# Hybrid attention, FFN and PLE layer: differential steps, the PLE gate and the order of three engines rearranged

## The chip, the core and the metric

The kernel runs on one core of one Trainium2 chip. The metric is device microseconds (us) of one execution. TensorE (PE in the profile) multiplies matrices, VectorE (DVE), ScalarE (ACT) and GpSimd (POOL) work on elements, SyncE (SP) and POOL issue DMA transfers. Each engine works through its own list of instructions in order, and semaphores make one wait for another.

## The reference

One layer on 512 tokens of 1024 features, all fp32. Cut to what matters:

```python
h = rms_norm(x, attn_norm_g); z = h @ w_in       # q, kv latents, rope key | diff q, k, v
x = x + concat[MLA heads (8 x 64), differential heads (4 x 128)] @ w_out
x = x + conv_ffn(rms_norm(x, ffn_norm_g), w_gate, w_up, conv_w, conv_b, w_down)   # D_FF = 2816
gate = jax.nn.sigmoid(rms_norm(x, ple_norm_g) @ w_ple_gate)                       # 1024 x 1024
x = x + gate * (p @ w_ple_proj)
...
probs = jax.nn.softmax(logits, axis=-1)          # differential head: two maps of one head
attn = (probs[:, :, 0] - lam * probs[:, :, 1])
return jnp.einsum('bhqk,bhkd->bhqd', attn, v_t)
```

Attention is causal by chunks of 64 tokens, so query block t (128 tokens) sees key blocks 0 to t.

## The kernel before

**Layout.** Everything is kept transposed: features on the 128 partitions, the 512 tokens on the free axis. The residual x is eight blocks of 128 features by 512 tokens. W_out, the FFN and the gate each give output blocks of that shape.

**Three matmuls for one.** For accuracy each operand is kept as a high half rounded to fp32r and a low half with the rest. mm3 (L188) issues three matmuls: high by high (L191), weight's high by activation's low (L192), weight's low by activation's high (L193). Weights are split when they have been loaded: ACT casts the high half (hi_, L1021), DVE subtracts for the low one (lo_, L1026; hl does both). split (L216) does the same for activations.

**Order.** PE runs the matmuls as the program's text lists them, written out by hand so that PE always has something ready. The other engines' order from MLA step 4 to the first FFN blocks is permuted afterwards by the table ISSUE (L69), one list of numbers for each of DVE, ACT, POOL and SP, which in_order (L228) applies to what has been traced since a mark. Behind that point the order is that of the text.

**The differential steps** (L960) go over 16 slots, head h and query block t. A slot issues logits two slots ahead (diff_qk, diff_soft, diff_comb), a filling product of W_out (pump, of FILL_DIFF's number of units), the transposes of its own P (probs_T, L591, tile pTd), P times V of the slot before (diff_pv, tile do), transposes of a later head's q and k (diff_T, tiles d0T and so on), and at some slots the split of a finished head's output (y_split, tile yT).

**The FFN** works through 22 blocks of 128 hidden features. From block 3 on, gate and up are computed together by a seven-product scheme on half blocks (gu_units, L1256; product, L1252): instead of eight products of half of the features by half of the tokens it takes seven, of sums of weights and sums of tokens, and adds the results. The sums of weights are made by an accumulating DMA on POOL's queue (w_sums, L1133; tile rS), the sums of tokens on DVE (tokens, L1169). Down products (down_units, L1336, tile dn) fill in between, and add_x (L738) adds each to x.

**The tail.** The last two groups of hidden blocks are multiplied by dn4 and dn5 (L1486, L1490), eight output blocks. As each block of x is ready, norm_in (L1481) splits it, times the gain, into h3h and h3l, and squares it for the norm (square, L1048: ACT squares, DVE sums into ss). Then the gate: pg (L1512) multiplies one output block, 8 feature blocks by 3 matmuls, 512 tokens wide, the last output block in two halves of 256. The first two output blocks take their first four feature blocks before the norm's matmul (L1538, with a square of ones, 512 wide; rms_v, L201, turns it into 1/rms in 11 DVE operations), since the factor 1/rms is only needed in ple_out (L1522): sg = pg times 1/rms, sigmoid on ACT, times the PLE projection ppi (loaded from DRAM, where an earlier stage wrote it), plus x, and out by DMA. Four 512 KB weight tiles of the gate are split early into FFN buffers (b1, b2), four late (pg_weights, L1509).

Of the kernel before, what the change touches and what calls it, by code (L numbers as in the profile page):

```python
# [128 lines left out]
def hybrid_block(ctx: ExitStack, tc: tile.TileContext, a: dict, out: bass.AP):  # L129
# [1308 lines left out]
    pump(2)  # L1438
    old, g = g, new
    for f in range(NPLAIN + 2, NF):  # L1440
# [13 lines left out]
        else:  # L1454
# [3 lines left out]
            pgw = []  # L1458
            for n, i in (("b1", 0), ("b2", 2)):
                h_, l_ = (ffn2.tile([P, 2, 1024], F32R, tag=n + j, name=f"pg{n}{j}") for j in "hl")  # L1460
                for j in range(2):
                    split(h_[:, j], l_[:, j], raw_w(a["w_pg"][i + j, 0], "rS", f"pg{i + j}", bufs=3))
                    pgw.append((h_[:, j], l_[:, j]))
# [170 lines left out]
```

## Time and profile before

| | us |
|---|---|
| median of 3 runs | 633.38 (633.19 to 633.41) |
| the profiled execution | 633.87 |
| its span (first to last instruction) | 632.1, mean granted clock 0.998 |
| busy: PE / PEld / DVE / ACT / POOL | 626.0 / 555.0 / 481.9 / 359.1 / 69.9 |
| moved by DMA | 82.63 MB |

PE is TensorE's matmuls, PEld its weight loads, which overlap them. A row of the trace gives an instruction's start, its length, its engine, its line, the operation, output and inputs by the program's tile names (their numbers left out), and in brackets how long the engine waited just before and for what. Lengths of neighbouring matmuls overlap, so the distance between starts says what one costs. A row of the windows gives the stretch, its length, then busy time and number of instructions of PE, PEld, DVE, ACT and POOL, then the mean granted clock, the DMA engines' busy share and GB/s.

### The profile page before, as it was taken

The numbers are of one execution on the slowest core, as the hardware profiler recorded it, in microseconds if no ns is written. First come the engines' busy times: TensorE is split into PE (matmuls) and PEld (weight loads), VectorE is DVE, ScalarE is ACT, GpSimd is POOL, SyncE is SP. The second block draws the span as 40 slices with busy tenths as digits, with TensorE's granted clock in tenths as the row PEclk, the third lists the DMA queues.
The fourth block names the chain that finished last, engine by engine and source line by source line (L and its number), as shares of the span: only waits on it lengthen the run. The fifth ranks groups of instructions, "written<-read, shape, count | busy, mean of one in ns | idle before, by whom it ended". The sixth has DMA issues, their size and how long they took to land.

```text
span 632.1 us, 10195 instructions
## 1 busy us (share of the span) xinstructions
PE 626.0 (99%) x3900; PEld 555.0 (88%) x3900; DVE 481.9 (76%) x870; ACT 359.1 (57%) x629; POOL 69.9 (11%) x94
## 2 busy tenths in 40 slices
...
GB/s 298 113 167 34 184 101 67 67 121 81 122 14 68 83 121 326 137 99 218 151 184 118 184 119 184 120 187 120 186 120 188 122 156 128 173 134 71 32 81 51
DMA packets 29912, 82.63 MB, mean 131 GB/s; under 512 B 3100, under 2 KB 4124, under 8 KB 29736
## 3 DMA queue, kind: packets, MB, share of 16 engines
...
q10 hardware_dynamic: 432, 0.49, 0.3%
...
## 4 chain that ended last, share of the span: by engine, by line
PE 98%; DMA 1%; ACT 0%; DVE 0%; ACTq 0%; issue 0%
PE dn L192 6%; PE dn L191 6%; PE dn L193 6%; PE gx L192 4%; PE gx L193 4%; PE gx L191 4%; PE g L191 4%; PE g L192 4%; PE g L193 4%; PE zd L191 4%; PE zd L193 4%; PE zd L192 3%; PE o L191 3%; PE u L191 2%; PE o L193 2%; PE o L192 2%
## 5 line engine op out<-in xcount | busy, mean ns | idle before, releaser
L1027 DVE TENSOR_TENSOR wSl<-rS,wSh 128x1024 fp32r<-128x1024 f32 x21 | 25.7, 1223 | 42.3 <-ACT wSh L1023 42.2
L191 PE MATMUL dn<-ah,hi_dn 128*128 128x512 f32 x144 | 56.3, 391 | 0.0
L192 PE MATMUL dn<-al,hi_dn 128*128 128x512 f32 x144 | 56.3, 391 | 0.0
L193 PE MATMUL dn<-ah,lo_dn 128*128 128x512 f32 x144 | 56.1, 389 | 0.0
L1136 POOL DMA_DIRECT2D rS<-in_w_gu x19 | 22.7, 1195 | 247.7 <-DVE cv L1304 129.1
L1023 ACT CAST wSh<-rS 128x1024 fp32r<-128x1024 f32 x21 | 22.0, 1048 | 37.3 <-PE gy L192 37.2
L191 PE MATMUL zd<-hi_d,xh 128*128 128x512 f32 x96 | 39.4, 411 | 0.0
L192 PE MATMUL zd<-lo_d,xh 128*128 128x512 f32 x96 | 37.6, 392 | 0.0
L739 DVE TENSOR_TENSOR x<-x,dn 128x512 f32<-128x512 f32 x44 | 29.8, 680 | 6.1 <-PE dn L193 6.1
L1023 ACT CAST wAh<-rA 128x1024 fp32r<-128x1024 f32 x21 | 22.1, 1052 | 20.0 <-DMA rA<-in_w_gu 12.3
L193 PEld LDWEIGHTS dn<-ah,lo_dn 128*128 128x128 f32 x144 | 27.1, 188 | 5.7
L1027 DVE TENSOR_TENSOR wTl<-rA,wTh 128x1024 fp32r<-128x1024 f32 x19 | 23.3, 1224 | 11.2 <-ACT wTh L1023 10.7
L191 PEld LDWEIGHTS dn<-ah,hi_dn 128*128 128x128 f32 x144 | 27.1, 188 | 5.1
L192 PEld LDWEIGHTS dn<-al,hi_dn 128*128 128x128 f32 x144 | 27.1, 188 | 5.0
L1027 DVE TENSOR_TENSOR wAl<-rA,wAh 128x1024 fp32r<-128x1024 f32 x21 | 25.6, 1217 | 4.5 <-ACT wAh L1023 4.5
L1307 ACT ACTIVATE cv<-cv 128x512 f32<-128x512 f32 x22 | 13.8, 630 | 25.6 <-DVE cv L1304 25.6
L191 PE MATMUL o<-yh,hi_o 128*128 128x512 f32 x64 | 26.8, 419 | 0.0
L192 PE MATMUL g<-b2l,wAh 128*128 128x256 f32 (+1 forms) x88 | 26.2, 298 | 0.0
L193 PE MATMUL g<-b2h,wAl 128*128 128x256 f32 (+1 forms) x88 | 26.2, 298 | 0.0
L191 PE MATMUL g<-b2h,wAh 128*128 128x256 f32 (+1 forms) x88 | 26.2, 298 | 0.0
L1527 ACT ACTIVATE sg<-sg 128x512 f32<-128x512 f32 (+1 forms) x9 | 5.3, 584 | 36.8 <-DVE sg L1526 36.8
L660 ACT ACTIVATE pm<-ml,sums,rq 128x128 f32<-128x128 f32 (+3 forms) x32 | 19.6, 617 | 9.8 <-DVE sums L636 6.1
...
## 6 DMA issues: line engine op xcount, KB each, us to landing
rA<-in_w_gu SPq DMA_DIRECT2D x22, 512.0 KB, 3.7
rS<-in_w_gu SPq DMA_DIRECT2D x22, 512.0 KB, 3.6
rS<-in_w_gu POOLq DMA_DIRECT2D x19, 512.0 KB, 6.0
raw_dn<-in_w_down SPq DMA_DIRECT2D x18, 512.0 KB, 5.8
raw_d<-in_w_d SPq DMA_DIRECT2D x12, 512.0 KB, 3.4
r<-in_w_gu SPq DMA_DIRECT2D x19, 256.0 KB, 5.8
raw_o<-in_w_out SPq DMA_DIRECT2D x8, 512.0 KB, 3.6
rS_pg<-in_w_pg SPq DMA_DIRECT2D x6, 512.0 KB, 4.1
```

What stands on the lines that cost most here:

```text
L191: TE.matmul(ps, xh, wh, start=first and i == 0, stop=False, skip_group_check=again)
L192: TE.matmul(ps, xh, wl, start=False, stop=False, skip_group_check=again)
L193: TE.matmul(ps, xl, wh, start=False, stop=last and i == n - 1, skip_group_check=again)
L660: S.activation(pm[c], ps[c], AF.Exp, bias=nm[:, c:c + 1], scale=r[:, c:c + 1], accum_out=sums[:, 1, c:c + 1])
L739: V.tensor_tensor(xb(b), xb(b), ps, op=ALU.add)
L1023: S.copy(h_, src)
L1027: V.tensor_tensor(l_, src, _f32(h_), op=ALU.subtract)
L1136: nc.gpsimd.dma_start(sums[f].rearrange("p (i c) -> p i c", i=2), a["w_gu"][f][:, :2048].rearrange("p (i c) -> p i c", i=2)[:, :, :512], a ...
L1307: S.activation(cv, cv, AF.Silu)
L1527: S.activation(sg, sg, AF.Sigmoid)
```

## The change

**The gate in seven products.** The gate's four pairs of output blocks (k and k + 4) are each computed by the scheme of the FFN. With the weight in four quarters, the tokens in two halves t1 and t2, and features in two halves (h1, blocks 0 to 3; h2, blocks 4 to 7), a pair takes the products named 11, 12, S2, S1, S3, S4 and 22, each four feature blocks by three matmuls, 256 tokens wide. 336 half matmuls take the place of 168 full and 48 half ones. The order on PE is: 11 of blocks 0 and 1, the norm's first part, 12 and 11 in turn for the rest, the norm's second part; then for each pair S2, S1, S3, S4, 22. Output block k is in pg, k + 4 in pu.

**What feeds it.** Host arrays hold w_pg in the layout of w_gu. For each k the sums of weights come by three accumulating transfers on POOL's queue behind loads on SP's: pg_sums (512 KB) makes the operand of S1 and S3, pg_mix (a load and two transfers of 256 KB, one after the other) that of S2 and S4, called t0 to t3. Weights are split twelve times at 1024 columns and four times at 512, in place of eight times at 1024. pg_tokens makes the sums of tokens: for each k four DVE operations on half blocks, two ACT casts and two DVE subtractions on full ones.

**The norm** uses norm_r and norm_b, which the first FFN norm has already: four matmuls of one column, a power on POOL, and one full matmul that spreads the result.

**The output.** Blocks 0, 1, 2, 4 and 5 are added into x by an accumulating DMA on POOL's queue; 3, 6 and 7 by DVE as before; 3 and 7, the last pair, go in two halves. ple_out's scalar -1 turns the sign of the upper blocks. ppi is loaded early (pp_in).

**The rest of the tail.** The last FFN block's product 22 now stands ahead of the last down unit (next(old), pump()); the last down weights are split into the tile btl.

**The differential steps.** P's transposes go ahead of the filling product, except at eight slots (early), and where no product is in the way; six slots change. P times V of the slot before moves to the slot's end. At slot (2,0), head 2 and query block 0, PE's rows before were (dl are logits, o the filling product, pTd P's transposes, do P times V):

```order
L193 MATMUL dl_2225<-st 128x384
L191 MATMUL o_2200<-yh_1857,hi_o_1948 128x512
L192 MATMUL o_2200<-yh2l,hi_o_1948 128x512
L193 MATMUL o_2200<-yh_1857,lo_o_1949 128x512
L191 MATMUL o_2200<-yh_1849,hi_o_1948 128x512
L192 MATMUL o_2200<-yh3l,hi_o_1948 128x512
L193 MATMUL o_2200<-yh_1849,lo_o_1949 128x512
L595 MATMUL pTd_2252<-ident,pmd 128x128
L817 MATMUL do_2119<-zd_1458,pt 128x128
```

And now (d0T are transposes of the next head's keys):

```order
L213 MATMUL dl_2225<-st 128x384
L615 MATMUL pTd_2245<-ident,pmd 128x128
L211 MATMUL o_2200<-yh_1857,hi_o_1948 128x512
L212 MATMUL o_2200<-yh2l,hi_o_1948 128x512
L213 MATMUL o_2200<-yh_1857,lo_o_1949 128x512
L211 MATMUL o_2200<-yh_1849,hi_o_1948 128x512
L212 MATMUL o_2200<-yh3l,hi_o_1948 128x512
L213 MATMUL o_2200<-yh_1849,lo_o_1949 128x512
L791 MATMUL d0T_2256<-ident,zd_789 128x128
```

The transpose of P has moved from behind the product to between the logits and the product, and P times V stands behind the next head's transposes.

**Two tables.** ISSUE has new numbers for DVE, ACT and SP, and ends where it did. A second table, ISSUE_TAIL, orders the tail on DVE (103 instructions), ACT (74), POOL (17) and SP (35). DVE's last rows before (pg, sg and ot are the gate's product, its sigmoid and the output, nr is 1/rms):

```order
L1526 TENSOR_TENSOR sg<-pg_6653,nr_6227 128x256
L1528 TENSOR_TENSOR sg<-sg,ppi 128x256
L1529 TENSOR_TENSOR ot<-x_1646,sg 128x256
L1526 TENSOR_TENSOR sg<-pg_6687,nr_6227 128x256
L1528 TENSOR_TENSOR sg<-sg,ppi 128x256
L1529 TENSOR_TENSOR ot<-x_1646,sg 128x256
```

And now (pg_6418 is block 3, pu_6916 block 7, ys the result of S1):

```order
L1638 SCALAR_TENSOR_TENSOR sg<-pu_6916,nr_6210 128x256
L1690 TENSOR_TENSOR pg_6418<-pg_6418,ys 128x256
L1640 TENSOR_TENSOR sg<-sg,ppi 128x256
L1646 TENSOR_TENSOR ot<-x_1646,sg 128x256
L1636 TENSOR_TENSOR sg<-pg_6418,nr_6210 128x256
L1640 TENSOR_TENSOR sg<-sg,ppi 128x256
L1646 TENSOR_TENSOR ot<-x_1642,sg 128x256
L1638 SCALAR_TENSOR_TENSOR sg<-pu_6916,nr_6210 128x256
L1640 TENSOR_TENSOR sg<-sg,ppi 128x256
L1646 TENSOR_TENSOR ot<-x_1646,sg 128x256
```

The end was one block in two halves, three operations each; now it is three half blocks, and the half that PE finishes last (the last three rows) stands behind all of block 3's second half.

ACT's last rows before:

```order
L1023 CAST wShpg_6547<-rS_pg_6545 128x1024
L222 ACTIVATE h3h<-x_1646,cols 128x512
L1056 ACTIVATE nsq<-x_1646 128x512
L1527 ACT_TABLE_LOAD
L1527 ACTIVATE sg<-sg 128x512 x7
```

Now, behind the last square (rS_t_6260 is t1, dhipgt_6608 its high half; pth are high halves of the token sums, hph, hpl and hq the sums):

```order
L1612 ACTIVATE pth<-hph_6286 128x512
L239 CAST dhipgt_6608<-rS_t_6260 128x1024
L1522 ACTIVATE hpl_6328<-x_1642,cols 128x512
L1614 CAST pth<-hq 128x512
L1625 COPY pg_6417<-px_6414 128x256
```

Where ACT had only sigmoids left, it now casts token sums and weights in turn, t1's cast among them.

The diff, cut:

```diff
 ISSUE = {
     mybir.EngineType.DVE: [
-        5, 0, 2, 6, 4, 3, 1, 7, 17, 8, 12, 14, 13, 18, 9, 10, 15, 11, 16, 19, 21, 22, 20, 23, 24, 25, 26, 27, 35, 29, 28, 30, 45, 31, 32, 33, 34, 44,
+        0, 5, 2, 1, 3, 4, 6, 7, 16, 9, 12, 11, 13, 14, 10, 15, 35, 8, 19, 20, 21, 22, 23, 24, 26, 27, 25, 17, 18, 29, 44, 30, 31, 32, 33, 34, 28, 45,
...
+ISSUE_TAIL = {
...
@@ differential steps @@
-        pump(FILL_DIFF[h][t])
+        early = t == 2 or (h, t) in ((0, 1), (1, 3), (DH - 1, 0), (DH - 1, 1))
+        if early:
+            pump(FILL_DIFF[h][t])
         df["pt", h, t] = probs_T(df.pop(("pm", h, t)), (t + 1) * P, f"d{h}{t}", True)
-        if i:
-            diff_pv(*dslots[i - 1])
+        if not early:
+            pump(FILL_DIFF[h][t])
...
+        if i:
+            diff_pv(*dslots[i - 1])
...
+    def pg_sums(k):
+        m = raw_w(a["w_pg"][k][:, 1536:2560], "rS", f"pgs{k}", bufs=3)
+        nc.gpsimd.dma_start(m.rearrange("p (i c) -> p i c", i=2), a["w_pg"][k][:, :2048].rearrange("p (i c) -> p i c", i=2)[:, :, :512], accum_op=ALU.add)
+        return m
...
-        pump(2)
+        pump(2 if new else 1)
...
-    w5 = [hl(raw_w(a["w_down"][LAST // 2, i], "rA", f"d5{i}", bufs=2), ("wT", "wS")[i], f"d5{i}") for i in range(2)]
+    mark = traced()
     next(old)
+    pump()
...
+    def pg_mix(k):
+        tag = "rS" if k < 2 else "rA"
+        m = tm[k] = raw_w(a["w_pg"][k][:, :1024], tag, f"t{k}", bufs=3 if k < 2 else 2)
+        nc.gpsimd.dma_start(m[:, :512], sums[k][:, 512:], accum_op=ALU.add)
+        nc.gpsimd.dma_start(m[:, 512:], m[:, :512], accum_op=ALU.add)
...
+    def pg_tokens(k):
+        p, q, x = hp_[k], t5("hq"), xb(k + K2)
+        hq_[k] = q
+        V.scalar_tensor_tensor(q[:, t2], x[:, t2], pcol(k + K2), p[:, t2], op0=ALU.mult, op1=ALU.subtract)
+        V.tensor_tensor(p[:, t2], p[:, t2], p[:, t1], op=ALU.subtract)
+        V.tensor_tensor(p[:, t1], p[:, t1], q[:, t2], op=ALU.add)
+        V.scalar_tensor_tensor(q[:, t1], x[:, t1], ncol[:, k:k + 1], p[:, t1], op0=ALU.mult, op1=ALU.add)
+        o = [y[:, k].rearrange("p i c -> p (i c)") for y in pt_]
+        S.activation(o[0][:, :T], p, AF.Copy, scale=-1.0)
+        V.scalar_tensor_tensor(o[1][:, :T], p, -1.0, _f32(o[0][:, :T]), op0=ALU.mult, op1=ALU.subtract)
+        S.copy(o[0][:, T:], q)
+        V.tensor_tensor(o[1][:, T:], q, _f32(o[0][:, T:]), op=ALU.subtract)
...
     def ple_out(b, ps, c0=0, c1=T):
...
+        if b % K2 < 2 or b == 2:
+            ot = xb(b)
+            nc.gpsimd.dma_start(ot, sg, accum_op=ALU.add)
+        else:
+            ot = dwn.tile([P, T], F32, tag=tag, bufs=8, name="ot")[:, :n]
+            V.tensor_tensor(ot, xb(b)[:, c0:c1], sg, op=ALU.add)
         nc.sync.dma_start(out[b * P:(b + 1) * P, c0:c1], ot)
...
+    p11(0)
+    p11(1)
+    pg_w(3)
+    norm_r()
...
+    for k in range(K2):
+        last = k == K2 - 1
+        s2(k)
+        s1(k)
+        s3(k)
+        if last:
+            ple_out(k, PG[k], 0, H2)
+            ple_out(k + K2, U[k], H2, T)
...
+        s4(k)
...
+        ple_out(k, PG[k], H2 if last else 0, T)
+        product(U[k][:, t1], PW[k]["22"], tp_[4], True)
+        ple_out(k + K2, U[k], 0, H2 if last else T)
+    in_order(mark, ISSUE_TAIL)
```

More of the change, by code (lines that the diff above doesn't have):

```diff
@@ L1457, in hybrid_block @@
             w4 = [hl(raw_w(a["w_down"][f0 // 2 + i, 1], "rA", f"d4{i}", bufs=2), "wA", f"d4{i}", bufs=2) for i in range(2)]
[L1458 to L1463, printed above, removed]
+            sums[0] = pg_sums(0)
         next(g)
@@ L1479, in hybrid_block @@
     nrm.pop("any")
+    pcol = lambda b: cols[:, C_PLE + b:C_PLE + b + 1]
+    hp_ = {}
     def norm_in(b):
-        split(h3h[:, b], h3l[:, b], xb(b), cols[:, C_PLE + b:C_PLE + b + 1])
+        h_, l_ = (x[:, b % K2] for x in (h1, h2)[b // K2])
+        split(h_, l_, xb(b), pcol(b))
+        if b < K2:
+            hp_[b] = dwn.tile([P, T], F32, tag="a" + "hl"[b % 2], bufs=8, name="hp" + "hl"[b % 2] + str(b))
+            S.activation(hp_[b], xb(b), AF.Identity, scale=pcol(b))
         square(b)
@@ L1494, in dn5, with pg_split, cut, pg_w @@
         norm_in(b)
+    def pg_split(raw, where, name):
+        pool, t, n = {"A": (ffn, "wA", 2), "T": (ffn, "wT", 1), "D": (dwn, "", 2)}[where]
+        h_, l_ = (pool.tile([P, 1024], F32R, tag=t + (i[0] if t else i), bufs=n, name=where.lower() + i + name) for i in ("hi", "lo"))
+        split(h_, l_, raw)
+        return h_, l_
+    def cut(w, *keys):
+        return {k: tuple(x[:, 512 * j:512 * j + 512] for x in w) for j, k in enumerate(keys)}
+    PW, tm, r22 = [{} for _ in range(K2)], {}, {}
+    def pg_w(k):
+        PW[k].update(cut(pg_split(raw_w(a["w_pg"][k][:, :1024], "rA", f"pg{k}", bufs=2), "D" if k < 2 else "A", f"pg{k}"), "11", "12"))
+    def pg_mix(k):
[3 more added lines that the diff above has]
+        nc.gpsimd.dma_start(m[:, 512:], m[:, :512], accum_op=ALU.add)
+    def pg_w2(k):
+        PW[k].update(cut(pg_split(tm[k], "D" if k % 2 else "T", f"pgt{k}"), "S2", "S4"))
+    def pg_w1(k):
+        PW[k].update(cut(hl(sums[k], "wS", f"pg{k}") if k < 2 else pg_split(sums[k], "A", f"pgs{k}"), "S3", "S1"))
+    def pg_w0(k):
+        if k == 0:
+            r22[0] = raw_w(a["w_pg"][k][:, 1024:1536], "r22", f"pg{k}", 512)
+        if k in (0, 3):
+            w = hl(r22[k], "w22", f"pg{k}", 512)
+        else:
+            w = [dwn.tile([P, 512], F32R, tag="al", bufs=8, name=f"w22{j}pg{k}") for j in "hl"]
+            split(*w, r22[k])
+        PW[k].update(cut(w, "22"))
+        if k + 1 < K2:
+            r22[k + 1] = raw_w(a["w_pg"][k + 1][:, 1024:1536], "r22", f"pg{k + 1}", 512)
     part = {b: bank("lg", f"dn4{b}") for b in (4, 5)}
+    pg_mix(0)
+    pg_w1(0)
     for b in (4, 5):
         dn4(part[b], b, False)
+    pg_w2(0)
+    pg_w0(0)
+    sums[1] = pg_sums(1)
+    pg_mix(1)
+    pg_w(0)
+    pg_w(1)
     for b in range(4):
         dn5(bank(("lg", "ob", "acc", "acc")[b], f"dn5{b}"), b, True)
+    sums[2] = pg_sums(2)
     for b in (4, 5):
@@ L1519, in pg_bank @@
-    def pg_bank(b):
-        return bank("acc" if b % 4 < 2 else "tp", f"pg{b}")
+    pt_ = kvp.tile([P, K2, 4, H2], F32R, tag="kv", name="pth"), ffn2.tile([P, K2, 4, H2], F32R, tag="btl", name="ptl")
+    tp_ = {i: tuple(x[:, :, j] for x in pt_) for j, i in enumerate((2, 1, 4, 3))}
+    hq_ = {}
+    def pg_tokens(k):
[10 more added lines that the diff above has]
+        V.tensor_tensor(o[1][:, T:], q, _f32(o[0][:, T:]), op=ALU.subtract)
@@ new lines, in hybrid_block, with p11, p12 @@
+    xs = [bank("acc", f"px{i}") for i in range(2)]
+    X = [xs[i // 2][:, i % 2 * H2:i % 2 * H2 + H2] for i in range(K2)]
+    PG = [bank("tp" if i < 2 else "lg", f"pg{i}") for i in range(K2)]
+    U = {}
+    h11, h21, h22 = tuple(x[:, :, t1] for x in h1), tuple(x[:, :, t1] for x in h2), tuple(x[:, :, t2] for x in h2)
+    def p11(k):
+        product(X[k], PW[k]["11"], h11, k % 2 == 1)
+        S.copy(PG[k][:, t1], X[k])
+    def p12(k):
+        product(PG[k][:, t1], PW[k]["12"], h21, True)
@@ L1522, in ple_out @@
     def ple_out(b, ps, c0=0, c1=T):
         n = c1 - c0
-        pp, sg, ot = (dwn.tile([P, T], F32, tag=t, bufs=8, name=i)[:, :n] for t, i in (("ah", "ppi"), ("al", "sg"), ("al", "ot")))
-        nc.sync.dma_start(pp, pps[b][:, c0:c1])
-        V.tensor_tensor(sg, ps[:, :n], nrm["r"][:, c0:c1], op=ALU.mult)
+        pp = ppi[b][:, c0:c1]
+        tag = "ah" if (b, c0) == (3, 0) else "al"
+        sg = dwn.tile([P, T], F32, tag=tag, bufs=8, name="sg")[:, :n]
+        if b < K2:
+            V.tensor_tensor(sg, ps[:, c0:c1], nrm["r"][:, c0:c1], op=ALU.mult)
+        else:
+            V.scalar_tensor_tensor(sg, ps[:, c0:c1], -1.0, nrm["r"][:, c0:c1], op0=ALU.mult, op1=ALU.mult)
@@ L1527, in ple_out @@
         S.activation(sg, sg, AF.Sigmoid)
         V.tensor_tensor(sg, sg, pp, op=ALU.mult)
-        V.tensor_tensor(ot, xb(b)[:, c0:c1], sg, op=ALU.add)
-        nc.sync.dma_start(out[b * P:(b + 1) * P, c0:c1], ot)
-    ps = [pg_bank(b) for b in range(4)]
-    for k in (0, 4):
-        for b in range(2):
-            pg(b, ps[b], k, k + 4)
-        if k == 0:
-            sps = bank("ob", "nr3")
-            TE.matmul(sps, ones, nrm["ss"], start=True, stop=True)
-            rms_v(nrm["r"], sps, T, D, (nrm["dg"], nr_[1][:, T:], nrm["ss"]))
@@ new lines, in ple_out, with pp_in @@
+        nc.sync.dma_start(out[b * P:(b + 1) * P, c0:c1], ot)
+    ppi = {}
+    def pp_in(b):
+        ppi[b] = dwn.tile([P, T], F32, tag="ah", bufs=8, name="ppi")
+        nc.sync.dma_start(ppi[b], pps[b])
+    pg_w(2)
+    p11(0)
[3 more added lines that the diff above has]
+    for k in range(K2):
+        pg_tokens(k)
+    for k in (1, 2):
+        pg_w0(k)
+    for k in range(K2):
+        pp_in(k)
+        pp_in(k + K2)
+    p12(0)
+    p11(2)
+    p12(1)
+    p11(3)
+    p12(2)
+    norm_b()
+    p12(3)
```

90 lines of the change are left out of this document (60 added, 30 removed), and 39 rows, old and new, of tables (ISSUE, ISSUE_TAIL).

## The prediction

> **What bounds the kernel now.** I read the page first, then the windows of the last 70 us, then PE's timeline where the change is.
>
> ```profile
> PE 626.0 (99%) x3900; PEld 555.0 (88%) x3900; DVE 481.9 (76%) x870; ACT 359.1 (57%) x629; POOL 69.9 (11%) x94
> PE 98%; DMA 1%; ACT 0%; DVE 0%; ACTq 0%; issue 0%
> 567.80:582.60 14.80, 14.80 (x67) 12.24 (x67) 14.09 (x21) 11.13 (x17) 0.00 (x0) 1.00 0.15 43
> 582.60:588.00 5.40, 5.40 (x25) 4.50 (x24) 5.02 (x7) 3.76 (x5) 0.00 (x0) 1.00 0.46 151
> 588.00:600.00 12.00, 12.00 (x52) 9.59 (x51) 9.79 (x15) 0.63 (x1) 0.00 (x0) 1.00 0.02 5
> 600.00:632.00 32.00, 27.48 (x144) 23.55 (x143) 14.28 (x24) 4.63 (x8) 0.00 (x0) 0.96 0.18 69
> ```
>
> PE is on 98% of the chain, so PE time saved is time saved, unless another engine falls behind. The second number of a window is PE's busy time, then PEld, DVE, ACT. From 567.8 to 588 DVE is busy 19.1 of 20.2 us, yet PE never pauses: there DVE has little left to give.
>
> **The gate's products.** The rows hold the start and length of each matmul; lengths overlap, so I price by the distance of starts.
>
> ```profile
> 559.37 0.28 PE L191 MATMUL u<-bth,w22h 128*128 128x256 f32 x1
> 560.80 0.40 PE L191 MATMUL dn<-ah,wAhd 128*128 128x512 f32 x1
> 561.03 0.40 PE L192 MATMUL dn<-al,wAhd 128*128 128x512 f32 x1
> 582.59 0.39 PE L191 MATMUL pg<-h3h,pgb1h 128*128 128x512 f32 x1
> 627.20 0.28 PE L193 MATMUL pg<-h3h,wSlpg 128*128 128x256 f32 x1
> 582.40:628.00 45.60, 44.60 (x216) 1.00 0.18 66
> 588.04 1.02 PE L1538 MATMUL nr<-nr,ones 128*128 128x512 f32 x2
> 588.50 0.80 PE L191 MATMUL pg<-h3h,pgb2h 128*128 128x512 f32 x1
> 589.13 0.39 PE L192 MATMUL pg<-h3l,pgb2h 128*128 128x512 f32 x1
> 229.24 0.95 PE L1105 MATMUL nr<-ones,nr 128*128 128x1 f32 x8
> 230.05 0.49 PE L191 MATMUL pp<-pk 128*128 128x512 f32 x1
> 230.37 0.40 PE L192 MATMUL pp<-pk 128*128 128x512 f32 x1
> ```
>
> The twelve half-width matmuls between 559.37 and 560.80 take 0.119 us each, a full one 0.23. The gate now has 216 matmuls (168 full, 48 half), and from its first start to its last 627.20 - 582.59 = 44.61 us pass, the norm's matmul in it. After: 7 products x 4 blocks x 12 = 336 half matmuls, 335 x 0.119 = 39.9. The norm is now four tiny ones (229.24 to 230.05, and 0.09 more on the next: 0.90) and one full (588.04 to 588.50, and 0.40 more on the next: 0.86).
>
> By the Trainium skill's page TensorE: Matmul & The Clock Gate (section Step-by-step: what each phase is for), a stream costs one cycle per moving column. Half the columns would then cost half of 0.23, and the 335 would take 38.5; the rows say 39.9, so seven eighths of the products don't give seven eighths of the time, and the row is used.
>
> **What DVE must deliver in time.** A half norm needs the last block's square; the third product (s3) needs all token sums. DVE's spacing, back to back:
>
> ```profile
> 567.83 0.69 DVE L739 TENSOR_TENSOR x<-x,dn 128x512 f32<-128x512 f32 x1 [4.68 <-PE dn L193]
> 579.14 0.75 DVE L223 SCALAR_TENSOR_TENSOR h3l<-x,cols,h3h 128x512 fp32r<-128x512 f32 x1
> 579.80 0.68 DVE L739 TENSOR_TENSOR x<-x,dn 128x512 f32<-128x512 f32 x1
> 580.40 0.69 DVE L1058 TENSOR_TENSOR nr<-nr,nsq 128x512 f32<-128x512 f32 x1
> 581.00 1.22 DVE L1027 TENSOR_TENSOR wAlpg<-rA_pg,wAhpg 128x1024 fp32r<-128x1024 f32 x1
> 582.14 0.75 DVE L223 SCALAR_TENSOR_TENSOR h3l<-x,cols,h3h 128x512 fp32r<-128x512 f32 x1
> 555.61 0.42 DVE L1277 TENSOR_TENSOR g<-g,y 128x256 f32<-128x256 f32 x1
> 555.94 0.42 DVE L1278 TENSOR_TENSOR u<-gx,y 128x256 f32<-128x256 f32 x1
> ```
>
> So 0.66, 0.60, 0.60, 1.14, and 0.33 for a half. DVE starts, as now, at 567.83 (block 0 of the down product). In its new order seven adds to x, seven low halves, five sums of squares and three weight splits (4.2 + 4.6 + 3.0 + 3.4 = 15.2) stand ahead of block 7's add: 583.05. That add, two sums of squares and two token halves end at about 585.65. PE is done with the two products it has first at 582.59 + 24 x 0.119 = 585.45, so the norm's tiny matmuls wait some 0.3 us; at full cover it would be 0.
>
> The whole stretch to the last token sum: 8 adds 4.8, 8 low halves 5.3, 7 sums 4.2, 5 weight splits 5.7, 16 token halves 5.6, 8 full token splits 5.0, the norm 0.8: 31.4 us, without a pause from 567.83 to 599.2. PE asks for it in s3 of block 0, after ten products: 582.59 + 0.3 + 0.90 + 0.86 + 14.3 + ten steps 1.2 = 600.15. Margin 0.9 us, so no wait; a cover of 3%.
>
> PE's last start then is 582.59 + 39.9 + 0.90 + 0.86 + 0.3 = 624.55: **2.65 earlier**.
>
> **The end.** Before, after the last matmul:
>
> ```profile
> 627.52 0.42 DVE L1526 TENSOR_TENSOR sg<-pg,nr 128x256 f32<-128x256 f32 x1 [1.08 <-PE pg L193]
> 627.98 0.42 ACT L1527 ACTIVATE sg<-sg 128x256 f32<-128x256 f32 x1 [2.46 <-DVE sg L1526]
> 628.42 0.42 DVE L1528 TENSOR_TENSOR sg<-sg,ppi 128x256 f32<-128x256 f32 x1 [0.48 <-ACT sg L1527]
> 628.88 0.42 DVE L1529 TENSOR_TENSOR ot<-x,sg 128x256 f32<-128x256 f32 x1
> ```
>
> DVE ends at 629.30, 2.10 after PE's last start: 0.32 to the first, three hops of 0.46, 0.42. Now look at DVE's last rows in the section on the change. The last three there, which finish PE's last product (22 of block 7's first half), stand behind the whole chain of block 3. Let the last matmul of s4 start at S; PE's last start is S + 1.43. The add to pg starts at S + 0.32, two queued halves follow, sg(pg) at S + 1.44, its sigmoid 1.90, product 2.36, ot 2.82, then sg(pu) 3.15, sigmoid 3.61, product 4.07, ot 4.53, done S + 4.95. That is 3.52 behind PE's last start, not 2.10: **1.42 given back**. If sg(pu) stood before the product it could start at S + 1.77, and nothing would be lost; that is the other bound.
>
> **What I cost at nothing, and its cover.** Twelve full and four half weight splits replace eight full ones: those ahead of 599 are in the 31.4; the rest are 7.5 us of DVE's about 22 behind 600, where 32 stand open (14.3 used now). ACT's half of each split is shorter than DVE's. The w_pg loads and their sums move 9.4 MB instead of 4.2, on DMA engines busy 2 to 18% there. The last FFN product goes ahead of one down product (twelve full matmuls, 2.7 us): PE's sum is the same, and the tile in which the last down weights are split comes free 2.7 us sooner, so their splits end near 564, ahead of their use at 566. Five output blocks are summed by accumulating DMAs on POOL, which spares DVE five full adds; the price is SP's queue: the last two output DMAs stand behind that of block 2, which waits for POOL's. DVE frees it at S - 1.7; landed 4.2 to 6.0 later it is ready by S + 4.3, ahead of the last ot at S + 4.95. Landed 9.8 later it would cost 3.
>
> **The differential steps.** PE's rows at step (2,0) stand in the section on the change: logits, P's transposes, then the product, where the product used to come second. Six steps get this. Nothing is removed, so only the seams change:
>
> ```profile
> 178.46 0.50 PE L191 MATMUL o<-yh,hi_o 128*128 128x512 f32 x1
> 178.79 0.39 PE L192 MATMUL o<-yh0l,hi_o 128*128 128x512 f32 x1
> 179.03 0.39 PE L193 MATMUL o<-yh,lo_o 128*128 128x512 f32 x1
> 194.50 0.66 PE L595 MATMUL pTd<-ident,pmd 128*128 128x128 f32 x4
> 195.00 0.83 PE L817 MATMUL do<-zd,pt 128*128 128x128 f32 x6
> 205.46 0.60 PE L722 MATMUL yT<-ident,yd 128*128 128x128 f32 x4
> 205.90 0.60 PE L595 MATMUL pTd<-ident,pmd 128*128 128x128 f32 x4
> ```
>
> A product behind logits starts with 0.33 instead of 0.24, 0.1 lost; transposes behind logits (194.50) take 0.50 instead of 0.44, 0.06 lost. The product's 0.1 is saved and the transposes' 0.06 paid, six times 0.04: **0.25**. P must be ready a product (1.5 us) earlier; DVE's and ACT's tables are moved with it, so I take no wait. If one step's cover goes, it costs up to 1.5.
>
> **Sum**: -2.65 + 1.42 - 0.25 = **-1.5 us** on a profiled execution of 633.87 (span 632.1): 632.4. The runs' median, 633.38, is 0.49 below that one: **631.9**.
>
> **Rivals.** 0.2% (1.27 us) is about what a measurement of this kernel can tell from no change.
>
> *DVE falls behind.* 31.4 us of work has 0.9 to spare. If its 52 instructions take 0.04 longer each (more waits per instruction), 2.1 is added, 1.2 reaches PE: 633.1, no change. For it: the window at 582.6 is 93% busy. Against: the spacings are measured, waits included. 0.20.
>
> *An accumulating DMA lands late; slower.* Weight sums for block 1 (t1) are added by two accumulating transfers one after the other on POOL's queue, and ACT's split of t1 stands ahead of the token splits, as ACT's rows in the section on the change show (the cast into dhipgt_6608, ahead of the token casts pth). If t1 is late, everything behind it on ACT waits, and so do DVE's token splits and s2.
>
> ```profile
> raw_dn<-in_w_down SPq DMA_DIRECT2D x18, 512.0 KB, 5.8
> ppi<-pps SPq DMA_DIRECT2D x7, 256.0 KB, 4.2
> DMA to landing us min/median/max: 5.7/6.0/9.8
> ```
>
> The last row is the 512 KB accumulate of the FFN (POOL, 19 times). t1's load leaves SP behind pg3's, which waits for DVE's second split (567.83 + 3.5 = 571.3): 571.7, landed 5.8 later, 577.5. Two accumulates of 256 KB at 4.2 (a plain load of that size) end at 585.9, at 6.0 at 589.5, at 9.8 at 597.1. DVE's split of t1 stands at about 589.6, so t1 is needed by 588.5. At 6.0 it is 1.0 late, hidden by DVE's margin; at 7.2 the change is slower by 0.2%; at 8.0 t1 lands 5.0 late, 4.1 reach PE: 636.0. 0.13.
>
> By the Trainium skill's page DMA: Bandwidth & Descriptors (section Anatomy of one DMA), a transfer costs 2.0 us and its bytes at 436 GB/s. That would be 2.6 each, t1 at 582.7, with no rival left; but the same rule makes 3.2 of the row that measures 6.0, so the row decides.
>
> *The new tables remove other waits.* Early in the FFN and at the end of attention DVE and ACT are reordered too; up to 0.7 more is gained: 631.2. 0.10.
>
> *The differential steps wait for P*, 1.5 once: 633.4. 0.05.
>
> **How the numbers follow.** The sum has 0.52. Its own bounds: no token or norm wait and 0.3 better, 631.2; half the DVE rival, 632.6. Range 630.9 to 634.0: it leaves out most of the late DMA (0.1) and some of the tables' gain. Faster by over 0.2% (below 632.1): two thirds of the sum's 0.52 and the tables' 0.10, 0.45. Same: the rest of the sum, DVE, the steps, 0.43. Slower: 0.12.
>
> **What would show it.** Right: PE's last start about 2.6 to 2.9 earlier and DVE's last ot 3.5 behind it; a pause of about 0.3 ahead of the norm's tiny matmuls; pTd behind dl and no pause there. Wrong: PE idle at s2 or s3 of block 0 with DVE (tokens) or a DMA into rS_t as releaser; t1 landing after 588.5; sg(pu) right behind PE.

## The result: 0.63% slower, and the profile after

The changed kernel took 637.12 us (median of 6 runs, 636.47 to 639.51) against 633.42 for the kernel before: ratio 1.0063, interval 1.0051 to 1.0076. 631.9 was forecast, in a range of 630.9 to 634.0. The profiled execution took 636.69, its span 634.6. The page, engines and chain:

```profile
PE 623.8 (98%) x4028; PEld 559.3 (88%) x4028; DVE 493.3 (78%) x900; ACT 379.8 (60%) x667; POOL 88.5 (14%) x112
PE 88%; DMA 4%; DVE 4%; ACT 2%; issue 1%; POOL 0%; ACTq 0%; DVEq 0%
```

PE has 2.2 us less to do, as the seven products promise, and yet it fell from 98% of the chain to 88%: it now waits for the other engines. The windows of the tail say where (length, then busy PE, PEld, DVE, ACT, POOL, clock, DMA share, GB/s):

```profile
582.60:588.00 5.40, 4.17 (x34) 3.88 (x33) 5.40 (x11) 3.36 (x8) 2.07 (x2) 1.00 0.79 170
588.00:600.00 12.00, 12.00 (x97) 11.52 (x97) 10.75 (x23) 7.52 (x14) 4.43 (x4) 1.00 0.69 152
600.00:610.00 10.00, 10.00 (x86) 10.00 (x85) 8.73 (x12) 7.84 (x13) 0.84 (x1) 1.00 0.97 230
```

A hole of 1.2 us in PE right at the gate's start, and DMA engines at 97% where they had been at 30%.

The two profiled executions can't be subtracted as they stand: the first kv product (ukv) starts at 32.80 before and at 31.95 after, ahead of any code that the change touches. Over all kernels of this study that start lay between 31.93 and 34.06. So all times below are counted from it. PE's timeline before, then after (first kv product, the gate's first matmul, PE's last):

```profile
32.80 0.40 PE L191 MATMUL ukv<-ukvh,latkh 128*128 128x512 f32 x1
```

```profile
31.95 0.40 PE L211 MATMUL ukv<-ukvh,latkh 128*128 128x512 f32 x1
...
582.94 0.28 PE L211 MATMUL px<-pb1h,dhipg 128*128 128x256 f32 x1
...
628.58 0.28 PE L213 MATMUL pu<-pth,w22lpg 128*128 128x256 f32 x1
```

| from the first kv product | before | after | difference |
|---|---|---|---|
| to the gate's first matmul | 549.79 | 550.99 | +1.20 |
| the gate, first to last start on PE | 44.61 | 45.64 | +1.03 |
| PE's last start to DVE's end | 2.10 | 3.23 | +1.13 |
| DVE's end to the span's end | 2.8 | 2.8 | 0 |

Together +3.36 us, near what the medians show (3.70); the two profiled executions differ by 2.82 only, since the changed kernel's began sooner.

**Ahead of the gate.** PE after, in the first seven-product blocks of the FFN:

```profile
282.62 0.28 PE L213 MATMUL gx<-bth,wTl 128*128 128x256 f32 x1
283.42 0.36 PE L211 MATMUL u<-bth,w22h 128*128 128x256 f32 x1 [0.52 <-ACT g L1295]
...
300.71 0.28 PE L212 MATMUL gx<-b1l,wAh 128*128 128x256 f32 x1
301.44 0.39 PE L213 MATMUL gx<-b1h,wAl 128*128 128x256 f32 x1 [0.45 <-DVE wAl L1051]
```

and DVE there:

```profile
281.91 0.43 DVE L1307 TENSOR_TENSOR g<-g,y 128x256 f32<-128x256 f32 x1 [0.81 <-ACT y L1306]
282.25 0.68 DVE L240 TENSOR_TENSOR al<-cv,ah 128x512 fp32r<-128x512 f32 x1
282.85 0.43 DVE L1308 TENSOR_TENSOR u<-gx,y 128x256 f32<-128x256 f32 x1
```

From 282.62 to 283.42 stand 0.80 instead of 0.12. Product 22 writes half of the PSUM bank u (a bank is a piece of the memory that PE writes its results to), and DVE's add to its other half (282.85) now stands behind a split (al) that used to come later; the add ends at 283.28, PE starts at 283.42. The bracket names ACT's copy of g, which ended within 0.02 of that; in the kernel before that copy ended 0.5 behind the start of PE's 22 and nothing waited, so it isn't the cause. At 300.71 the low half of a weight, wAl, stands on DVE behind another weight's low half, wSl, which used to come after it, and PE stands 0.61. At the FFN's norm PE waits 0.36. There the split on DVE beside POOL's power (r) is a longer one, and the power ended later. Before, then after:

```profile
230.33 0.69 DVE L1027 TENSOR_TENSOR w22l<-r,w22h 128x512 fp32r<-128x512 f32 x1
230.46 1.44 POOL L199 TENSOR_TENSOR r<-rs_m,mhalf 128x4 f32<-128x4 f32 x1 [5.14 <-DVE rs_m L198]
```

```profile
229.13 1.23 DVE L1061 TENSOR_TENSOR wTlpp<-rS_pp,wThpp 128x1024 fp32r<-128x1024 f32 x1
229.29 1.94 POOL L219 TENSOR_TENSOR r<-rs_m,mhalf 128x4 f32<-128x4 f32 x1 [5.13 <-DVE rs_m L218]
```

In both the power ends 0.87 or 0.88 behind the split. All seven kernels with the new order here have 1.94, the other nine 1.43 or 1.44. The three waits, 1.65 in all, are the table's price.

**In the gate.** PE after, at its two largest holes:

```profile
584.25 0.28 PE L213 MATMUL px<-pb1h,dlopg 128*128 128x256 f32 x1
585.77 0.39 PE L211 MATMUL px<-pb1h,dhipg 128*128 128x256 f32 x1 [1.24 <-ACT pg L1625]
...
618.57 0.28 PE L213 MATMUL pg<-pb2h,tlopgt 128*128 128x256 f32 x1
619.53 0.38 PE L211 MATMUL pu<-pth,w22hpg 128*128 128x256 f32 x1 [0.68 <-DVE pu L1696]
```

ACT after:

```profile
584.20 0.63 ACT L1080 ACTIVATE nsq<-x 128x512 f32<-128x512 f32 x1 [0.25 <-DVE x L759]
584.74 0.71 ACT L242 ACTIVATE pb2h<-x,cols 128x512 fp32r<-128x512 f32 x1
585.36 0.36 ACT L1625 COPY pg<-px 128x256 f32<-128x256 f32 x1
...
608.35 1.28 ACT L1639 ACT_TABLE_LOAD   x1
609.65 0.63 ACT L1639 ACTIVATE sg<-sg 128x512 f32<-128x512 f32 x1
...
616.83 1.05 ACT L239 CAST dhipgt<-rA_t 128x1024 fp32r<-128x1024 f32 x1 [1.90 <-DMA rA_t<-rA_t]
```

DVE after:

```profile
610.31 0.69 DVE L1640 TENSOR_TENSOR sg<-sg,ppi 128x512 f32<-128x512 f32 x1 [1.04 <-ACT sg L1639]
610.92 0.42 DVE L1696 TENSOR_TENSOR pu<-px,ys 128x256 f32<-128x256 f32 x1
...
617.90 1.23 DVE L240 TENSOR_TENSOR dlopgt<-rA_t,dhipgt 128x1024 fp32r<-128x1024 f32 x1 [3.49 <-ACT dhipgt L239]
619.05 0.43 DVE L1696 TENSOR_TENSOR pu<-px,ys 128x256 f32<-128x256 f32 x1
...
630.04 0.42 DVE L1638 SCALAR_TENSOR_TENSOR sg<-pu,nr 128x256 f32<-128x256 f32 x1
...
631.39 0.42 DVE L1646 TENSOR_TENSOR ot<-x,sg 128x256 f32<-128x256 f32 x1
```

Product 11 of block 1 shares a PSUM bank with that of block 0, and can start only when ACT has copied block 0 out. The copy takes 0.36 us, but on ACT it stands behind the last block's square and split, which wait for the last add to x: 1.4 lost. By the Trainium skill's page PSUM — Partial Sum Buffer (section PSUM bank collisions raise a hardware error), PSUM has to be guarded by bank and not by address. The trace agrees in so far as this kernel waits by bank: the 1.40 is there although the two halves have no column in common; no run here shows what would happen without the wait. Ahead of three of the four products 22 PE waits again, 0.76, 0.84 and 0.39, for DVE's work on the other half of the same bank. In the second pair DVE stood at a sigmoid that came behind a table load; in the third it stood 3.49 at the split of t3, whose last accumulating transfer had been issued at 610.07 and landed 6.7 later:

```profile
rA_t<-rS_pgs POOLq DMA_DIRECT2D x1, 256.0 KB, 6.4
rA_t<-rA_t POOLq DMA_DIRECT2D x1, 256.0 KB, 6.7
```

The wait of the third pair is this execution's: e4, e5, e7 and e9 below have the same order there and t3 as it is, and their traces have no wait ahead of that 22 at all. Their t3 landed 30.4 to 32.8 us behind the gate's first start, here 33.8. In e7, DVE's split of t3, then PE's first row of that 22, which follows the row before it at 0.12:

```profile
616.06 1.23 DVE L240 TENSOR_TENSOR dlopgt<-rA_t,dhipgt 128x1024 fp32r<-128x1024 f32 x1 [1.17 <-ACT dhipgt L239]
```

```profile
618.83 0.28 PE L211 MATMUL pu<-pth,w22hpg 128*128 128x256 f32 x1
```

So 0.84 of the gate's loss is order and a late transfer together; in e5, e7 and e9 the gate takes 44.72 to 44.74, which is 2.8 over the forecast and not 3.7.

### The profile page after: what moved, and what is told of

It reads as the page before. It is cut to its first block, busy times and chain, and to the rows that moved or that the text cites. A ratio compares the mean times of both kernels' runs of the same rounds, so it can differ in the third digit from the quotient of the medians.

```text
span 634.6 us, 10597 instructions
## 1 busy us (share of the span) xinstructions
PE 623.8 (98%) x4028; PEld 559.3 (88%) x4028; DVE 493.3 (78%) x900; ACT 379.8 (60%) x667; POOL 88.5 (14%) x112
## 2 busy tenths in 40 slices
DMA packets 34026, 91.30 MB, mean 144 GB/s; under 512 B 3500, under 2 KB 4524, under 8 KB 33848
## 4 chain that ended last, share of the span: by engine, by line
PE 88%; DMA 4%; DVE 4%; ACT 2%; issue 1%; POOL 0%; ACTq 0%; DVEq 0%
PE dn L212 5%; PE dn L211 5%; PE dn L213 5%; PE gx L213 4%; PE gx L212 4%; PE gx L211 4%; PE g L213 4%; PE g L212 4%; PE g L211 4%; PE zd L211 4%; PE zd L213 3%; PE zd L212 3%; PE o L211 2%; PE o L213 2%; PE u L211 2%; PE o L212 2%
## 5 line engine op out<-in xcount | busy, mean ns | idle before, releaser
L1047 ACT CAST wTh<-rA 128x1024 fp32r<-128x1024 f32 x19 | 19.9, 1049 | 11.2 <-PE g L212 8.8
```

Of the source, the lines that this page charges most:

```text
L1047: S.copy(h_, src)
```

## The experiments

Theory: the loss is the order in DVE's and ACT's queues, at places where PE's next product needs a bank that they hold. Rivals: late accumulating transfers; all of it in the gate. Beside each median stands the ratio to the kernel before on the same chip with its interval. Each trace is of one execution. Over the 15 kernels the median's distance from before and the trace's, counted from the first kv product, differ by -0.4 to 2.1 us, so an edit worth less than that is read from the trace's waits and not from the median.

**e1_front and e2_tail: one half of the change each.** e1 takes only the steps and ISSUE:

```diff
-        pump(FILL_DIFF[h][t])
+        early = t == 2 or (h, t) in ((0, 1), (1, 3), (DH - 1, 0), (DH - 1, 1))
...
 ISSUE = {
...
```

> The kernel before with the new differential steps and the new numbers of ISSUE, its old gate kept. Theory (queues): the steps give 0.33 (after's trace: from the first o to the last do PE is 0.33 quicker), but the new order costs PE 0.33 at the FFN's norm and 1.2 at 282.6 and 300.7, where adds to PSUM stand behind weight splits on DVE: 633.4 - 0.33 + 1.5 = 634.6. Rival (the whole loss sits in the gate, the steps gain and the table is neutral): 633.1.

Measured 635.75, 1.0034 (1.0022 to 1.0046), 1.1 above the 634.6 expected. Its trace has the three holes of the changed kernel (0.37, 0.68, 0.62), and reaches the gate 551.01 from the first kv product, after's 550.99. So a third of the loss has nothing to do with the gate; "the front is neutral" falls. The median is 0.9 above the 1.3 that the trace accounts for.

e2 is the rest: the changed kernel with the old steps and the old ISSUE.

> The changed kernel with the old differential steps and the old ISSUE; only the gate, its norm, its loads and ISSUE_TAIL are new. Theory (queues, in front and gate): 637.1 - 1.2 = 635.9. Rival (front neutral): 637.4.

Measured 637.19, 1.0064 (1.0052 to 1.0077): hardly less than the whole change, and the expected 635.9 was missed. The trace: PE is at the gate at 549.88, 1.1 sooner than in the changed kernel, but the gate took 46.12 instead of 45.64, with other holes (0.79 ahead of an S3, 1.27 ahead of a 22). The parts don't add in this pair of traces, and an earlier PE is not the reason: e5 comes to the gate sooner still, has no hole ahead of that S3 and only 0.76 ahead of that 22. In e2 ACT stood for a late load of a weight, with the copy that PE's S3 needed behind it:

```profile
607.34 0.62 ACT L239 CAST w22hpg<-r_pg 128x512 fp32r<-128x512 f32 x1 [3.08 <-DMA r_pg<-in_w_pg]
607.87 0.36 ACT L1676 COPY pg<-px 128x256 f32<-128x256 f32 x1
```

The load landed 5.9 us after its issue; in the changed kernel ACT waited 0.97 for it. So e2's time says nothing on the front's third; e1 and e5 show it.

**e3_nomix23: no sums t2 and t3.** The kernel leaves out that part of the gate.

```diff
-        nc.gpsimd.dma_start(m[:, :512], sums[k][:, 512:], accum_op=ALU.add)
-        nc.gpsimd.dma_start(m[:, 512:], m[:, :512], accum_op=ALU.add)
+        if k not in (2, 3): ...
```

> The changed kernel without the four accumulating transfers that make t2 and t3 (the plain quarter weights are split in their place, so the gate of pairs 2 and 3 is left uncomputed in that part). If late transfers are the cause, all three waits ahead of 22 go (0.76, 0.84, 0.39): 635.1, and runs differ less than 636.5 to 639.5. If order in the queues is, only the wait of the third pair goes, behind t3's split: 637.1 - 0.84 = 636.3; the one of the second pair stays, since DVE waits there for a sigmoid behind a table load.

Measured 637.11, 1.0057 (1.0045 to 1.0069). The 0.84 ahead of the third pair's 22 went, the 0.76 and 0.39 stayed (0.76 and 0.38), and PE's part of the gate fell to 44.73. That the two stayed speaks for the queues. That the 0.84 went says little, since it is also gone in e4, e5, e7 and e9, where t3 is made as before. The time did not follow: the span ended 3.66 behind DVE, not 2.78 (see e7).

**e4_banks: products of blocks 0 and 1 in two banks.**

```diff
-    X = [xs[i // 2][:, i % 2 * H2:i % 2 * H2 + H2] for i in range(K2)]
+    X = [xs[i % 2][:, i // 2 * H2:i // 2 * H2 + H2] for i in range(K2)]
```

> The changed kernel with the first-product sums of blocks 0 and 1 in two PSUM banks instead of two halves of one (blocks 0 and 2 share one, 1 and 3 the other), so that product 11 of block 1 needn't wait for ACT's copy of block 0. Simple sum: the 1.4 of waiting at 584.4 goes, 0.4 comes back as a wait for the norm's sum: 636.1. Queues: PE is 1.0 earlier only up to the first 22, and waits that much longer there, because DVE's chain behind the tokens has not moved: 637.0.

Measured 637.57, 1.0061 (1.0044 to 1.0077). In the trace the hole of 1.39 is gone, a wait of 0.28 for the norm has come, as the prediction had it, and the gate takes 44.11, 1.5 less. But 0.84 of the 1.5 is the third pair's wait, which e5, e7 and e9 lack too; against their 44.7 the two banks gave 0.6 and not the simple sum's 1.0, and 0.34 came back as waits for the token splits in the first pair's S2. That execution began 2.1 later than after's, and the median shows nothing.

**e5_ffn_old: the old order from the FFN's norm on.** DVE's list from place 244, ACT's from 140 and SP's from 22 are before's. One of the places on DVE:

```diff
+L1061 TENSOR_TENSOR wTlpp<-rS_pp,wThpp 128x1024
 L759 TENSOR_TENSOR x<-x,o 128x512
 L759 TENSOR_TENSOR x<-x,o 128x512
+L759 TENSOR_TENSOR x<-x,o 128x512
+L759 TENSOR_TENSOR x<-x,o 128x512
 L1051 TENSOR_TENSOR wAl<-rA,wAh 128x1024
-L759 TENSOR_TENSOR x<-x,o 128x512
-L759 TENSOR_TENSOR x<-x,o 128x512
```

> The changed kernel, gate, steps and ISSUE_TAIL as they are, but from the FFN's norm on ISSUE takes the numbers of before (the differential steps keep the new ones). Theory (the new order of the FFN's start makes PE wait 0.36 at the norm, 0.68 and 0.61 at the first seven-product blocks; its steps are 0.33 quicker): PE reaches the gate 1.5 sooner, counted from the first kv product on; the time follows by 0.6 to 1.5, since e2 showed that the gate's DVE chain gives part of an earlier start back: 635.6 to 636.5. Rival (these waits come from the steps, not from the table): the waits stay, 637.1.

Measured 636.54, 1.0041 (1.0026 to 1.0056). The first kv product and the gate's first matmul:

```profile
32.76 0.40 PE L211 MATMUL ukv<-ukvh,latkh 128*128 128x512 f32 x1
...
582.20 0.28 PE L211 MATMUL px<-pb1h,dhipg 128*128 128x256 f32 x1
```

549.44: 1.55 sooner than the changed kernel and 0.35 sooner than before. The three waits of the front are gone: they came from the table. (The gate's 44.74 is less than the changed kernel's because t3 landed in time.)

**e6_order: adds ahead of splits.** DVE, with the other four places alike:

```diff
 L1640 TENSOR_TENSOR sg<-sg,ppi 128x512
+L1696 TENSOR_TENSOR pu2<-px1,ys 128x256
 L240 TENSOR_TENSOR dlopgt3<-rA_t3,dhipgt3 128x1024
-L1696 TENSOR_TENSOR pu2<-px1,ys 128x256
```

> The changed kernel with five places of ISSUE_TAIL changed: the adds to pu of pairs 1 and 2 go ahead of a product with ppi and of t3's split, sg(pu) of pair 3 ahead of an output add; on ACT the copies of py and px of pair 2 go around t3's cast. Theory (queue order): the waits ahead of 22 in pairs 1, 2 and 3 (0.76, 0.84, 0.39) shrink to less than 0.2 each, up to 1.6 sooner at PE's last start, 635.5 to 636.0. Rival (data late: t2 and t3 are needed then anyway): the waits move to S2 of pairs 2 and 3 and the time stays 637.1.

Measured 637.93, 1.0070 (1.0058 to 1.0083), and not the 635.5 to 636.0 expected. The holes shrank to 0.43, none and 0.19, and the gate to 44.20, 1.44 less; nothing waited at S2. The edit's own part is the second and the last pair's, 0.5 against the 44.7 of e5, e7 and e9; t3 landed early here (30.9 behind the gate's start), so the new order at t3 was not put to the test. And the span ended 4.75 behind DVE.

**e7_end: the last sg(pu) ahead.**

```diff
 L1636 TENSOR_TENSOR sg<-pg3,nr 128x256
+L1638 SCALAR_TENSOR_TENSOR sg<-pu3,nr 128x256
 L1640 TENSOR_TENSOR sg<-sg,ppi 128x256
```

> The changed kernel with the last sg(pu) on DVE ahead of the product and the add of block 3's second half (its buffers come from the tag of ppi). From after's trace: sg(pu) at 628.9 instead of 630.04, last ot at 630.2 instead of 631.39: 1.2 sooner, 635.9. Rival (the last output transfers, queued on SP, set the end): 0.2 or less, 637.0.

Measured 637.94, 1.0069 (1.0054 to 1.0085). DVE was done 2.33 behind PE instead of 3.23, and the span ended 4.76 behind DVE instead of 2.78: the rival. POOL's last accumulate (block 2's output) and SP's last transfers:

```profile
624.93 0.84 POOL L1643 DMA_DIRECT2D x<-sg  x1 [2.02 <-DVE sg L1640]
```

```profile
628.09 2.04 SPq L1647 DMA_DIRECT2D out<-x  x2
630.23 1.73 SPq L1647 DMA_DIRECT2D out<-ot  x2
```

The second out<-x is block 2's, issued at 629.80, when the accumulate of 624.93 has landed (4.86 later). The last two outputs stand behind it. That is the cover which the prediction named and found sufficient; in e6, where the same accumulate took 6.3 us to land, it was gone as well.

**e8_all: e4 to e7 together.**

> The changed kernel with all four: two banks (e4), old FFN order (e5), the five places (e6), the end (e7). If the parts add up (1.0 to 1.5, 1.5, 1.6, 1.2): 631.3 to 632, faster than before's 633.5 by 0.2 to 0.35%. If DVE's chain behind the tokens, saturated from 568 to 610, becomes the bound: 633 to 634.5, no better than before.

Measured 635.70, 1.0039 (1.0025 to 1.0053), above both values expected. PE's part is there (gate at 549.36, 43.95 long), but the accumulate landed 6.4 after its issue and the span ended 5.75 behind DVE:

```profile
x<-sg POOLq DMA_DIRECT2D x1, 256.0 KB, 6.4
```

**e9_end_add and e10_all_add: block 2 added by DVE** (e7 and e8 with this edit):

```diff
-        if b % K2 < 2 or b == 2:
+        if b % K2 < 2:
...
+            ot = sg if b == 2 else dwn.tile(...)
```

> e7 (sg(pu) earlier at the end) with block 2's output added by DVE instead of by an accumulating transfer. In e7's trace DVE was done 0.9 earlier than in the changed kernel, but the span ended 4.76 behind DVE instead of 2.78: block 2's accumulate landed 4.86 after its issue, its output transfer stood on SP ahead of the last two, and they left late. Theory (that queue took the gain): the end is 2.8 behind DVE again, 1.9 sooner than e7, 635.9. Rival (output transfers are slow there by themselves): 637.5 or more, as e7.

> e8 (all four edits) with the same change at block 2. e8's span ended 5.75 behind DVE. Theory: 2.8 behind DVE, so 2.9 sooner than e8, 632.8; against before that is 0.8 quicker at most, 598.5 against 599.3 from the first kv product on, so within 0.2% of before. Rival (late transfers elsewhere hold PE): 634.5 or more.

e9 636.49, 1.0048 (1.0036 to 1.0060); e10 634.53, 1.0017 (1.0008 to 1.0026). Both spans end 2.8 behind DVE again, so the output queue is shown. In time each gave some 1.2 to 1.5 rather than 1.9 and 2.9. e10 is within 0.2% of before, as expected, but not ahead: its DVE add stands in front of the last pair's 22, which waits 0.89 there. Its profiled execution (633.14) lies near the 632.8 expected, its median at the rival's 634.5. Against the changed kernel's 1.0063 (1.0051 to 1.0076) e10's 1.0017 (1.0008 to 1.0026) is clear of noise: order, banks and one add took back about 2.7 of the 3.7 us.

**e11_all_sig: the table load out of the way** (a sigmoid of one column, early, added to e10).

```diff
+    S.activation(warm[:, :1], ones[:, :1], AF.Sigmoid)
```

> e10 with a sigmoid of one column on ACT between two copies of the first products, so that the table load (1.28) lies there and not ahead of the first sigmoid of the output. Theory (DVE's product with ppi waits 1.04 for that sigmoid and the 22 of pair 1 stands behind it): the wait ahead of that 22 (0.43 in e8) goes, 632.4. Rival: the second table has to be loaded again for the copies, or the load delays the copy of block 3: no gain, 632.8 or more.

Measured 634.59, 1.0007 (0.9994 to 1.0021). The hole of 0.43 went. The median did not move (632.4 was expected). In the profiled run, the slowest of twelve, t3 came late, landing 34.3 behind the gate's start: 1.86 lost at one 22, where DVE's add waited for ACT's copy behind the cast of t3. So e6's order had moved the wait for a late t3 from DVE to ACT and not removed it.

**e12_steps: the steps alone**, with before's order from the FFN's norm on and before's gate.

> The kernel before with the new differential steps and the new ISSUE up to the FFN's norm, from there on its old numbers; old gate. In e5's trace, which has the same front, the first kv product to the gate took 0.35 less than before's (549.44 against 549.79). Theory (the steps gain what the prediction said, the front's loss is all in the FFN's part of the table): 633.2 to 633.4, PE at the gate 0.35 sooner. Rival (steps neutral): 633.6.

Measured 633.15, 0.9995 (0.9986 to 1.0003): PE is 0.33 sooner at the end of the steps and still so at 301.3, but there it waits 0.44 (0.16 before, 0.12 in e5), which leaves 0.05 at the gate. The interval holds 1, so no gain is shown.

**e13_all_pool and e14_all_nomix: t2 and t3 added by POOL, or left out** (e11 with POOL's add for block 2's output):

```diff
+            if k < 2:
+                nc.gpsimd.dma_start(dst, src, accum_op=ALU.add)
+            else:
+                G.tensor_tensor(dst, dst, src, op=ALU.add)
```

> e11 with the four sums of t2 and t3 and the output of block 2 added by POOL itself (a 128x512 add takes 1.67 there in before's trace) instead of by accumulating transfers, which landed 3.3 to 8.2 behind their issue. Theory (what is left of the loss, and the spread of e11's runs from 632.3 to 636.5, is t3's chain of transfers): t3 is ready some 7 sooner, the wait of 1.86 ahead of pair 2's 22 goes and the one of 0.89 in pair 3 shrinks; 632.3 to 632.8, faster than before by 0.1 to 0.2%, runs within 1.5. Rival (POOL's adds hold DVE up, or the spread comes from the first loads): 633.5 or more, spread as in e11.

> e13 without the sums of t2 and t3 altogether (the plain quarter weights are split in their place, so that part of the gate of pairs 2 and 3 is left out). Theory: as e13 within 0.3, 632.2 to 632.8, runs within 1.5, since neither waits for t3. Rival (the spread comes from elsewhere): runs still 3 or 4 apart.

e13 639.27, 1.0086 (1.0073 to 1.0099), the slowest of all; e14, without these sums, 633.20, 0.9998 (0.9988 to 1.0008). In e13 POOL's adds hold DVE up. POOL, then DVE:

```profile
591.99 1.28 POOL L1560 TENSOR_TENSOR rA_t<-rA_t,rS_pgs 128x512 f32<-128x512 f32 x1
...
595.36 1.73 POOL L1560 TENSOR_TENSOR rA_t<-rA_t 128x512 f32<-128x512 f32 x1
```

```profile
592.03 1.79 DVE L1132 TENSOR_TENSOR nr<-ident,r 128x512 f32<-128x512 f32 x1 [0.93 <-POOL r L219]
...
594.81 2.57 DVE L1612 TENSOR_TENSOR hpl<-hpl 128x256 f32<-128x256 f32 x1
```

The half add took 2.57 instead of 0.41 and ended 0.3 behind POOL's add, and the gate grew to 48.51. The Trainium skill's page SBUF — State Buffer (section SBUF: two separate sides) has it that GpSimd and a DVE operation with two SBUF inputs lock each other out of a shared port pair for a whole instruction; the trace agrees. e14's trace has no wait over 0.29 left in the gate but the 0.40 at the norm's second part, and the gate takes 43.06 instead of before's 44.61. That profiled run is the fastest of its twelve. The kernel still isn't measurably faster than before, and its 12 runs lie 3.2 apart (631.74 to 634.95), against e11's 4.1. So t3's transfers alone are not what makes runs differ. What they cost is not shown by e14: it also has POOL add block 2, which removes the 0.89 of e10 and e11 at the last 22, and its interval overlaps e11's.

## Why the prediction was wrong, point by point

- **The price of the products held.** Half-width matmuls follow each other at 0.12 (582.94 to 584.25 in eleven steps), and PE has 2.2 us less to do.
- **The step that failed is the end of the part on DVE: "PE's last start then is 582.59 + 39.9 + 0.90 + 0.86 + 0.3 = 624.55".** It took PE to wait for nothing but the norm. Measured in the changed kernel: 45.64 from first to last start instead of 41.96. The 3.7 are 1.5 at the shared bank, 2.26 ahead of three products 22 (0.94 of them at the third pair, where t3 landed late in this execution), 0.2 at the norm's second part, less the 0.3 which the first hole covered. I had summed DVE's work up to the token sums, and checked that it was done in time; I had not looked, at each place where PE comes back to a bank, at what stands in DVE's and ACT's queue ahead of the operation that frees it. e4 removed the first hole, of which 0.6 stayed gained, and e6 took 0.5 off the second and the last pair's, by bank and order alone; the third pair's needs t3 in time.
- **The margin of DVE was used up.** 0.9 was given, on 31.4 us "without a pause". DVE's last token sum ended 18.0 behind the gate's first start in the changed kernel and 17.6 in e4, where 16.6 was forecast. The work was sized well; the pauses were missing: 0.76 and 0.50 for casts on ACT in the changed kernel, 0.93 for POOL's power in e4. There the power took 3.48 instead of 1.40, ending 0.9 behind the last of four operations that DVE ran one after the other beside it. In the changed kernel the first hole hid this; in e4 PE was held 0.10, 0.14 and 0.10 in S2 of the first pair.
- **The end was right**: DVE's last add ended 3.23 behind PE's last start, 3.52 was forecast. Block 2's output on SP, which I costed at nothing, cost nothing in this execution: its accumulate landed 4.8 us after its issue, at 630.5, ahead of DVE's end at 631.8. But the cover was thin. Over the kernels it took 4.7 to 6.4 us, and with a quicker DVE (e7, e8) or a slower landing (e6) it set the end.
- **The steps came out near the forecast, in part by luck**: -0.25 forecast, -0.32 measured to the end of the last P times V, with no wait for P. Up to the start of that last group the seams gave 0.18; the rest came inside it, where the weight load's wait for ACT's copy got shorter, which is not a seam. Before, then after:

```profile
207.31 0.97 PEld L817 LDWEIGHTS do<-zd,pt 128*128 128x128 f32 x8 [0.34 <-ACT pt L598]
```

```profile
206.14 0.97 PEld L837 LDWEIGHTS do<-zd,pt 128*128 128x128 f32 x8 [0.20 <-ACT pt L618]
```

- **The tables were a rival in one direction only.** "Up to 0.7 more is gained" had no counterpart; measured, 1.55 was lost (e5 against the changed kernel). I had compared the rows of the FFN's start and not timed them: an add and a weight's low half each moved behind another split, and a longer split beside the norm's power, cost 0.68, 0.61 and 0.36.
- **The late accumulate was sought at t1 and sat at t3.** t1 landed at 587.97, within the 585.9 to 589.5 given, and cost nothing. t3 is the end of four transfers in a row, 592.05 to 616.76, on DMA engines which the change itself filled to 97%; "busy 2 to 18% there" was read from a trace in which these transfers did not exist, and the bytes were summed too low: 9.4 MB instead of 4.2 would be 5.2 more, the pages have 91.30 against 82.63, 8.7 more. A late transfer cost 0.84 in the changed kernel's profile, 1.86 in e11's, and the late weight in e2's has a gate 1.4 longer beside it (46.12 against 44.7), so the rival was underrated, though the rest of the loss is there without it.

Open: what makes runs of one kernel differ by 2 to 4 us. The first kv product's start alone moved by 2.1 between the profiles, in code that all kernels share; behind it the time between DVE's end and the span's (2.8 to 5.8) and t3's landing moved too. The spread goes with the new gate: 29 runs of before lie 2.2 apart and 11 of e12 1.3, the 11 and 12 of e5, e10, e11 and e14 3.0 to 4.5. Why e1's median is 0.9 above its trace's account is open as well. No version was measurably faster than before; the best is e12.
